# Loading the last tile of x in transfers of 5, 121 and 2 partitions instead of 5, 120 and 3

## Chip, core and metric

The kernel runs on one core of one Trainium2 chip. Five engines work side by side in a core: TensorE (PE) multiplies, VectorE (DVE), ScalarE (ACT) and GpSimd (POOL) do the elementwise work, and SyncE (SP) issues transfers. Sixteen DMA engines carry the data between the chip's main memory and the core's memory, whose 128 rows are called partitions. The metric is the device time of one execution in microseconds; the time before is the median of 3 runs.

## The reference

```python
batch, m, k, n = 16, 512, 1024, 768
x         = randn(batch, m, k)   # float32
weight    = randn(k, n)          # float32
sub_value = randn(batch, m, n)   # float32

def reference(x, weight, sub_value):
    return (np.matmul(x, weight) - sub_value).astype(np.float32)
```

With batch and m joined there are 8192 rows of x, that is 64 tiles of 128 rows. A tile of x is 128 partitions of 1024 float32, 4 KB in each partition and 512 KB in all. A tile of sub_value or of the output has 3 KB in each partition.

## The kernel before

The kernel casts each tile of x to float16 (ScalarE), transposes it (on TensorE, and for some pairs of tiles on VectorE), multiplies it by the weight (TensorE), subtracts sub_value from the product (VectorE) and stores the result. Loads and stores are listed in one order, with the kind (x, w for the weight, s for sub_value, o for the output), the first tile and the number of tiles:

```python
TRANSFERS = [
    ('x', 0, 1), ('w', 0, 1), ('x', 1, 1), ('w', 1, 1), ('x', 2, 1), ('w', 2, 1),
    # ... cut ...
    ('o', 8, 8), ('o', 16, 8), ('s', 40, 8), ('x', 48, 8), ('s', 48, 8), ('x', 56, 7), ('p', 63, 1),
    ('o', 24, 8), ('o', 32, 8), ('s', 56, 8), ('o', 40, 8), ('o', 48, 8), ('o', 56, 5),
    ('o', 61, 2), ('o', 63, 1),
]

PARTS = (120, 125), (0, 120), (125, 128)
```

All kinds but 'p' are issued by SyncE, each as one transfer over 128 partitions. Kind 'p' is tile 63 of x. GpSimd issues it, as three transfers over the ranges of partitions in PARTS, in that order, and each has a semaphore of its own:

```python
            if kind == "p":
                here, there = x_ring[:, at % NX], view(x_flat, at, 1)[:, 0]
                waits, landed["x", at] = [(counter["cast"], cast_at[at - NX]), *landed["x", at - 1]], []
                for low, high in PARTS:
                    sem = tc.alloc_semaphore(f"part{low}")
                    pool.add(lambda low=low, high=high, here=here, there=there: nc.gpsimd.dma_start(
                        out=here[low:high], in_=there[low:high], max_dma_last_dim=2048,
                    ), waits, (sem, 16))
                    landed["x", at].append((sem, 16))
                continue
```

GpSimd waits for the cast that frees the place in the ring of x tiles and for the load of x tiles 56 to 62, and then issues the three. The cast of tile 63 waits for all three semaphores:

```python
    def cast(mi):
        # ... cut ...
        waits = list(landed["x", mi])
        # ... cut: choice of the float16 buffer ...
        act.add(lambda: nc.scalar.copy(out=to, in_=x_in), waits, count("cast"))
```

The transfers that follow in SyncE's queue, the stores ('o') and the last load of sub_value ('s', 56), do not wait for tile 63. The end of the kernel is the arrival of the last store, ('o', 63, 1), at its semaphore, and of the other stores still open.

Of the kernel before, what the change touches and what calls it, by code (L numbers as in the profile page):

```python
# [35 lines left out]
    ('o', 61, 2), ('o', 63, 1),  # L36
]

PARTS = (120, 125), (0, 120), (125, 128)


class Queue:
# [65 lines left out]
def kernel(  # L108
# [134 lines left out]
    def issue():  # L243
        nonlocal known
        while todo:
# [14 lines left out]
# [5 lines that stand above are left out]
# [306 lines left out]
```

## Time and profile before

| | before |
|---|---|
| device time, median of 3 runs | 210.65 us (210.53 to 210.82) |
| span of the profiled execution | 208.6 us |
| data moved | 87.08 MB, mean 417 GB/s |
| TensorE clock granted, mean | 0.993 |
| GpSimd's three issues (line L265) | mean 668 ns each, 162.4 to 163.9 us |
| tile 63, from issue to landing | 6.8, 14.7 and 15.8 us |

The page is of one execution. It gives the busy time of each engine and, in rows of 40 digits, the busy share of each fortieth of the span (9 is 90% or more). Transfers are counted by packet, one packet being a contiguous run moved by one DMA engine; q1 is the queue of SyncE's transfers, q0 that of GpSimd's. Groups of instructions stand with their count, their mean duration and the idle time ahead of them; issues of transfers stand with the kilobytes of each and the time from issue to landing. In a row of the timeline, the first number is the start, the second the duration, both in microseconds.

### The profile page before, as it was taken

Reading aid. Unit: us, or ns where it says so; the run is one execution under the profiler, and the core shown is the slowest. Engines: PE = TensorE matmul, PEld = TensorE weight load, DVE = VectorE, ACT = ScalarE, POOL = GpSimd, SP = SyncE. Lnnn points to the kernel's source line nnn. Section 1 sums busy time; section 2 is a strip of 40 time slices with the busy share of each in tenths; the row PEclk is TensorE's granted clock in tenths of the full one; section 3 lists DMA queues with packets and bytes.
Section 4 is the critical chain, followed back from the end, with each engine's and each line's share of the span. In section 5 each row is a group of like instructions: output and inputs, shape, how many; then the busy total and the mean of one; then the engine's idle time right before and its main releaser. Section 6 shows DMA issues by size and latency. Waiting matters only on the chain.

```text
span 208.6 us, 2617 instructions
## 1 busy us (share of the span) xinstructions
PE 195.2 (94%) x1234; PEld 75.4 (36%) x700; DVE 128.1 (61%) x224; ACT 109.0 (52%) x113; POOL 3.0 (1%) x10
## 2 busy tenths in 40 slices
PE   6899699969999999999999999999999999999960
PEld 0233244324434433443443443344344344344310
DVE  2233224975993895597399389469739938942330
ACT  2655659506573761854745676183574746516300
POOL 1000000000000000000000000000000300000000
PEclk9999999999999999999999999999999999999997
DMA  6999999999999999999999999999999999999993
GB/s 204 421 428 429 437 423 431 449 435 427 424 440 446 371 443 433 444 421 411 455 440 427 415 429 448 430 452 404 424 441 428 433 432 423 443 424 433 421 418 155
DMA packets 5685, 87.08 MB, mean 417 GB/s; under 512 B 689, under 2 KB 689, under 8 KB 2097
## 3 DMA queue, kind: packets, MB, share of 16 engines
q1 hardware_dynamic: 5472, 86.51, 97.3%
q0 software_dynamic: 208, 0.52, 0.6%
q14 instruction: 4, 0.02, 0.0%
q8 instruction: 1, 0.02, 0.0%
HBM read 61.87 MB, written 25.17 MB: 417 GB/s over the span
## 4 chain that ended last, share of the span: by engine, by line
PE 75%; DMA 13%; DVE 6%; SPq 3%; issue 1%; DVEq 0%
PE po_b L200 67%; DMA so_ring<-in_sub_value_dram 13%; PE pt_b L348 8%; DVE xtp_b L381 3%; DVE so_ring L430 2%; SPq L311 2%; SPq L275 1%; SPq L566 0%; DVEq L61 0%; SPq L140 0%
## 5 line engine op out<-in xcount | busy, mean ns | idle before, releaser
L200 PE MATMUL po_b<-w_sb,xt_b 128*128 128x384 f16 x704 | 126.0, 326 | 0.9 <-DVE w_sb L278 0.8
L430 DVE TENSOR_TENSOR so_ring<-po_b,so_ring 128x768 f32<-128x768 f32 x64 | 60.7, 957 | 58.9 <-PE po_b L200 39.8
L361 ACT COPY xt_b<-pt_b 128x1024 f16<-128x1024 f16 x44 | 44.5, 1012 | 64.7 <-PE pt_b L348 63.8
L381 DVE STREAM_TRANSPOSE xtp_b<-x16p_b 32x256 f32<-32x256 f32 x144 | 62.7, 435 | 2.3
L200 PE MATMUL po_b<-w_sb,xtp_b 128*128 128x384 f16 x320 | 61.3, 326 | 1.8 <-DVE xtp_b L381 1.7
L410 PEld LDWEIGHTS <-xt_b 128*128 128x128 f16 x352 | 34.4, 98 | 58.4 <-issue 55.2
L330 ACT CAST x_b<-x_ring 128x1024 f16<-128x1024 f32 x46 | 47.2, 1048 | 5.5 <-DMA x_ring<-in_x_dram 5.5
L348 PE MATMUL pt_b<-ident,x_b 128*128 128x128 f32 x184 | 47.6, 274 | 1.9 <-ACT x_b L330 1.9
L348 PEld LDWEIGHTS pt_b<-ident,x_b 128*128 128x128 f32 x184 | 25.3, 141 | 45.0 <-issue 36.3
L330 ACT CAST x16p_b<-x_ring 128x1024 f16<-128x1024 f32 x18 | 18.8, 1046 | 14.8 <-DMA x_ring<-in_x_dram 14.8
L410 PEld LDWEIGHTS <-xtp_b 128*128 128x128 f16 x160 | 15.7, 98 | 20.3 <-issue 18.3
L278 DVE CAST w_sb<-so_ring 128x768 f16<-128x768 f32 x8 | 4.1, 557 | 12.0 <-DMA so_ring<-in_weight_dram 12.0
L200 PE MATMUL po_b<-idle_x,idle_w 128*128 128x512 f16 x26 | 7.7, 443 | 1.7 <-POOL idle_x L180 1.7
L265 POOL DMA_DIRECT2D x_ring<-in_x_dram x3 | 2.0, 668 | 136.7 <-DMA x_ring<-in_x_dram 136.7
L361 ACT COPY xtp_b<-pt_b 128x1024 f16<-128x1024 f16 x2 | 2.0, 1012 | 2.4 <-PE pt_b L348 2.4
L330 ACT ACT_TABLE_LOAD x1 | 1.3, 1283 | 0.9 <-SPq L140 0.9
L440 PEld LDWEIGHTS <-idle_w 128*128 128x128 f16 x4 | 0.4, 100 | 1.7 <-POOL idle_x L180 1.7
L189 DVE TENSOR_TENSOR ident<-along,across 32x32 f32<-32x32 f32 x4 | 0.7, 183 | 0.1
L181 DVE MEMSET ones<- 128x32 f32 x1 | 0.1, 85 | 1.0 <-SPq L140 1.0
L180 POOL MEMSET idle_x<- 128x512 f16 x1 | 0.5, 531 | 0.0
L489 POOL MEMSET mark<- 128x1 f32 x1 | 0.1, 99 | 24.0 <-ACT xtp_b L361 24.0
L512 ACT CAST stub<-ident 128x1 f16<-128x1 f32 x2 | 0.4, 194 | 0.0
(8 smaller groups left out, 1.2 us busy)
## 6 DMA issues: line engine op xcount, KB each, us to landing
so_ring<-in_sub_value_dram SPq DMA_DIRECT2D x7, 3072.0 KB, 24.2
out_dram<-so_ring SPq DMA_DIRECT2D x7, 3072.0 KB, 26.6
x_ring<-in_x_dram SPq DMA_DIRECT2D x4, 4096.0 KB, 21.6
x_ring<-in_x_dram SPq DMA_DIRECT2D x2, 2048.0 KB, 27.2
x_ring<-in_x_dram SPq DMA_DIRECT2D x1, 3584.0 KB, 21.9
so_ring<-in_weight_dram SPq DMA_DIRECT2D x4, 768.0 KB, 8.8
x_ring<-in_x_dram SPq DMA_DIRECT2D x1, 3072.0 KB, 28.3
x_ring<-in_x_dram SPq DMA_DIRECT2D x2, 1024.0 KB, 24.8
```

What stands on the lines that cost most here:

```text
L189: dve.add(lambda here=here: nc.vector.tensor_tensor(out=ident[here, here], in0=along[here], in1=across[here], op=mybir.AluOpType.is_equal, ...
L200: return nc.tensor.add_instruction(mybir.InstMatmult(name=nc.get_next_instruction_name(), engine=full.engine, ins=list(full.ins), outs=lis ...
L265: pool.add(lambda low=low, high=high, here=here, there=there: nc.gpsimd.dma_start(out=here[low:high], in_=there[low:high], max_dma_last_di ...
L275: sp.add(lambda st=st, at=at: nc.sync.dma_start(out=st, in_=w_c[at]), then=(sem, 16))
L278: lambda at=at, r=r, st=st: nc.vector.tensor_copy(out=w_sb[:, at, r], in_=st[:, r]),
L311: sp.add(lambda here=here, there=there: nc.sync.dma_start(out=here, in_=there), waits, (sem, 16))
L330: act.add(lambda: nc.scalar.copy(out=to, in_=x_in), waits, count("cast"))
L348: pe.add(lambda: nc.tensor.transpose(words, from_, ident), waits, count("turn") if last else None)
L361: act.add(lambda: nc.scalar.copy(out=to, in_=pt_b[:, b]), waits, count("evac"))
L381: dve.add(lambda: nc.vector.transpose(xt[b * Q : (b + 1) * Q, :, a * Q : (a + 1) * Q], x16[a * Q : (a + 1) * Q, :, b * Q : (b + 1) * Q],), ...
L410: pe.add(lambda weights=weights: nc.tensor.ldweights(weights, tile_position=(0, 0)), [w for w in waits if w[0] in ready])
L430: dve.add(lambda: nc.vector.tensor_tensor(out=o, in0=po[:, :, :NS], in1=o, op=mybir.AluOpType.subtract), [*landed["s", mi], (counter["mul" ...
```

## The change

The first of GpSimd's three transfers still has 5 partitions, 121 to 125 instead of 120 to 124. The second has 121, 0 to 120, instead of 120. The third has the last 2 instead of 3. The same 128 rows of 4 KB are loaded, in the same order of issue, with the same waits. The ranges determine how the rows of tile 63 are divided over the DMA engines, and that division is what the change is about.

```diff
-PARTS = (120, 125), (0, 120), (125, 128)
+PARTS = (121, 126), (0, 121), (126, 128)
```

## The prediction

> **What bounds the kernel now.** I read the page first: the share of each engine, then the row of DMA slices and the DMA queues.
>
> ```profile
> span 208.6 us, 2617 instructions
> PE 195.2 (94%) x1234; PEld 75.4 (36%) x700; DVE 128.1 (61%) x224; ACT 109.0 (52%) x113; POOL 3.0 (1%) x10
> ...
> DMA  6999999999999999999999999999999999999993
> ...
> q1 hardware_dynamic: 5472, 86.51, 97.3%
> q0 software_dynamic: 208, 0.52, 0.6%
> ```
>
> TensorE is busy for 94%, but the DMA row shows 9 in every slice except the first and the last, and SyncE's queue q1 alone fills 97.3% of 16 engines' time. GpSimd's queue q0, the one that is changed, has 208 packets and 0.6%. To see which of the two bounds holds the end, I read the timeline's last rows, then the DMA issues, and then DMA from 204 us to the end, cut into 40 slices of 0.125 us.
>
> ```profile
> 201.51 0.96 DVE L430 TENSOR_TENSOR so_ring<-po_b,so_ring 128x768 f32<-128x768 f32 x1 [1.64 <-PE po_b L200]
> ...
> out_dram<-so_ring SPq DMA_DIRECT2D x1, 384.0 KB, 4.8
> ```
>
> ```profile
> DMA  9898988882614131211111100000000000000000
> GB/s 418 344 516 344 418 369 344 344 344 98 270 74 197 49 123 74 98 74 74 74 74 49 49 0 0 0 0 0 0 0 0 0 0 0 0 0 0 0 0 0
> ```
>
> Computing ends at 201.51 + 0.96 = 202.47 us. The last store, 384 KB, lands 4.8 us after its issue, although at the 430 GB/s of the middle it is worth only 0.9 us: it stands behind stores that are still queued. In the last view all 16 engines run until about 205 us (nine slices at 8 or 9), and then fewer and fewer of them, at last one alone, until the 23rd slice, at 206.9 us. So the end is **the DMA engine with the longest backlog**. The other engines' early finish buys nothing. (The chain of waits names TensorE for 75%; it follows the last addition back and doesn't show this backlog.)
>
> The trace's packet records have start, duration and size, but no engine. I followed the 16 engines through them: on a busy engine each packet starts 3 to 4 ns before its predecessor's end. The last packets of the 16 end from 204.8 to 207.0 us: twelve by 205.8, then 206.2, 206.70, 206.76, 207.00. The lag is old: the last engine landed its share of the transfer of x tiles 40 to 47 at 114.9 us, when the middle one stood at 113.2. It isn't made up, since no engine is ever idle.
>
> Next, the part that changes: the three issues of GpSimd, DMA in the stretch from 160 to 180 us, and the cast that uses tile 63.
>
> ```profile
> x_ring<-in_x_dram POOLq DMA_DIRECT2D x1, 480.0 KB, 14.7
> x_ring<-in_x_dram POOLq DMA_DIRECT2D x1, 20.0 KB, 6.8
> x_ring<-in_x_dram POOLq DMA_DIRECT2D x1, 12.0 KB, 15.8
> ```
>
> ```profile
> DMA packets 578, 8.54 MB, mean 427 GB/s; under 512 B 124, under 2 KB 124, under 8 KB 252
> ...
> q0 software_dynamic: 208, 0.52, 6.6%
> ```
>
> ```profile
> 191.20 1.05 ACT L330 CAST x_b<-x_ring 128x1024 f16<-128x1024 f32 x1
> ```
>
> Issued from about 162 to 164 us, the three land by 179.6 us at the latest (landing of the 3-row part). The cast is at 191.2 us and has no idle time before it, so there are over 11 us of slack. The latency of the transfer doesn't matter. **What matters is which engine carries how many of its 128 rows.**
>
> **What the skill says.** The Trainium skill, "DMA: Bandwidth & Descriptors", section "Why a DMA increments its semaphore by 16 and not by 1", says that a transfer runs on k engines, the largest k up to 16 that divides the slowest dimension; for GpSimd's transfers they are k consecutive engines from a round-robin cursor. It also gives an exception: some direct copies from GpSimd take k = 16 with the partitions divided by 16 and rounded up on each engine. The section "Queues, rings and completion order" says that an engine alternates between its queues packet by packet.
>
> The trace agrees with the alternation: while q0 is active, a 24,576-byte packet of q1 and a row of q0 take turns, and the step grows from 908 to 1,063 ns. It agrees with the cursor as well. q0's 208 packets are 128 rows of 4,096 bytes, 48 of 4 bytes (3 transfers x 16 engines, the semaphore) and 32 of 8 bytes, which I call fillers. 32 = 11 + 8 + 13: one for each engine that has no row in the 5-row part, eight on the one engine without rows in the 120-row part, one for each without a row in the 3-row part. Following the packets, this one engine, X, carries one row of the 5, then eight fillers, then one row of the 3. That is a cursor: engines c to c+4, then the fifteen from c+5 on, which leaves out c+4 = X, then c+4 to c+6. So X carries 2 rows, six engines carry 9, and nine carry 8: 2 + 54 + 72 = 128. X is also a slow engine: many of its 24,576-byte packets take 945 ns where 912 is the median, so leaving it out helps.
>
> **The change part by part.** Nothing is added on any compute engine, and the bytes are the same. Only the division over engines moves. A row in the alternation costs 1,063 - 908 = 0.155 us of its engine, a filler about 914 - 908 = 0.006 us. 121 is 11 x 11, and here the skill's two rules part:
>
> - **By the divisor rule**, k = 11. Engines c+5 to c+15 carry 11 rows each, c to c+4 carry none of the 121; the cursor returns to c, and the 2-row part goes to c and c+1. Against before, the nine engines with 8 rows get +3 rows = 3 x 0.155 = +0.465 us. Engines c+5 and c+6 go from 9 to 11, +0.31 us. Engines c to c+4 carry 1 or 2 rows and end about 1 us earlier, except X, which goes from 2 rows to 1, -0.155 us.
> - The last engine before (207.00 us) has 8 rows and 2 fillers in the records, so it is one of the nine: 207.00 + 0.465 = 207.46 us. The one at 206.76 had 9 rows and can go either way; X, at 206.70, is near 206.55. So the end is +0.465 us: 210.65 + 0.465 = **211.1 us**. As the stalls that make an engine late fall differently in each run and now five engines out of 16 are relieved, +0.3 is as possible as +0.46.
>
> The 121 rows need 11 steps of 1.063 us instead of 8, 3.2 us longer: they land near 181 us instead of 177.8, still 10 us before the cast.
>
> **The rivals.**
>
> 1. *The rounded-up division.* 121 / 16 rounds up to 8 rows on each engine: 15 engines with 8, and the sixteenth, which had none, with one. If this too follows the cursor, the sixteenth is X, which then loses the row of the last part, while c+5 and c+6 get the two rows: X carries 2, six carry 9, nine carry 8, exactly as before, and the time stays at **210.65 us**. For it: 120 rows on 15 engines are what this rule gives as well (120 / 8), and the skill's exception is about direct copies, which these are. Against it: with k = 16 fixed from the lowest engine, the parts of 5 and 3 would not both meet X; the trace shows that the 120-row part moved the cursor by 15.
> 2. *X ends last.* X is slow and has stalls of its own (packets of 1,236 and 1,395 ns late in this trace), and ends only 0.3 us before the last. In runs where X is last, one row less makes the end 0.15 us earlier, until the engines with 11 rows pass it: **210.5 to 210.9 us**.
> 3. *The tile comes too late.* If 121 rows went through one engine, 121 x 1.063 = 129 us would hold up the cast: over **300 us**. Only a row count without a usable divisor would do that, and 121 has 11. I give this 1%.
>
> **Range and chances.** The divisor rule has about 65%, the rounded-up division 35%: 0.65 x 0.45 + 0.35 x 0 = +0.3 us, so 210.95 us. The range goes from 210.5 (rival 1 or 2, with runs spread as before, 210.53 to 210.82) to 211.4 (0.465 and 0.3 us of stalls on top). 2% would be 4.2 us. No part of this reaches it but rival 3, so within 2% has 0.975; slower gets 0.015 for rival 3 and what I have not seen, faster 0.01.
>
> **What the changed profile would show.** q0's packets decide between the rules. With k = 11 there are 128 rows, 48 semaphore packets and 11 + 5 x 11 + 14 = 80 fillers, **256 in all**; with rounding up, 11 + 7 + 14 = 32 fillers, **208** as before. With k = 11 the 121-row part should take some 3 us longer to land than 14.7, and the thin tail after the first engines' end should be longer by some 0.4 us, beginning earlier. Casts, additions and matmuls should keep their durations and TensorE its end near 201.5 us. The prediction is wrong if the end moves with 208 packets on q0, if the cast of tile 63 waits for its transfer, or if k = 11 shows and the time doesn't rise: then the last engine isn't one of the eleven, or isn't what sets the end.

## The result, and the profile after

| | before | after |
|---|---|---|
| device time, median | 210.64 us (210.53 to 210.82) | 211.84 us (211.60 to 212.03) |
| ratio to before | | 1.0055, 95% interval 1.0038 to 1.0073 |
| tile 63, three parts, issue to landing | 6.8, 14.7, 15.8 us | 6.6, 18.7, 19.7 us |
| last addition ends | 202.47 us | 203.62 us |

The change costs 1.2 us, by the interval 0.8 to 1.5 us. That is within 2%, but above the predicted range (210.5 to 211.4 us), with more than twice the predicted rise of 0.46 us for this division.

First the page of the kernel after: the span, the engines, the row of DMA slices and the two queues.

```profile
span 210.2 us, 2617 instructions
PE 195.8 (93%) x1234; PEld 75.5 (36%) x700; DVE 128.2 (61%) x224; ACT 108.9 (52%) x113; POOL 3.0 (1%) x10
...
DMA  6999999999999999999999999999999999999993
...
q1 hardware_dynamic: 5472, 86.51, 97.2%
q0 software_dynamic: 256, 0.53, 0.7%
```

The busy times of the engines are those of before within 0.6 us, and q1 moved the same packets. q0 has 256 packets instead of 208: 128 rows, 48 of the semaphores and 80 fillers. This is the signature that the prediction gave to the divisor rule with k = 11. The issues agree (the last two numbers of a row are the size and the median time from issue to landing):

```profile
x_ring<-in_x_dram POOLq DMA_DIRECT2D x1, 484.0 KB, 18.7
x_ring<-in_x_dram POOLq DMA_DIRECT2D x1, 20.0 KB, 6.6
x_ring<-in_x_dram POOLq DMA_DIRECT2D x1, 8.0 KB, 19.7
```

The 121 rows land 4.0 us later than the 120 rows did, where 3.2 us was predicted. No cast waits for them. The timeline has the cast of tile 63 at 192.35 us, and by then the tile has been there for some 8 us:

```profile
192.35 1.05 ACT L330 CAST x_b<-x_ring 128x1024 f16<-128x1024 f32 x1
```

Then the end, in the same view as before: DMA from 204 to 209 us in 40 slices of 0.125 us.

```profile
DMA  8885979499967979596653243110000000000000
GB/s 369 344 344 221 664 295 565 197 516 442 467 246 320 369 295 442 221 418 270 271 221 148 98 172 123 49 49 0 25 25 25 25 25 25 25 25 0 0 0 0
```

The engines stop one after the other from about 206.5 us on, and in slices 29 to 36 the rate is 25 GB/s, that of a single engine, until 208.5 us. It is the engine that ended last before, known by its lag in the packet records; I call it **L**. In these records, followed from packet to packet as in the prediction, the next-latest engines end at 207.35 us.

Where does L lose its time? The table has the time at which L finished its share of each transfer in the two profiled executions (us):

| transfer | before | after | difference |
|---|---|---|---|
| x tiles 56 to 62 | 161.85 | 162.59 | +0.74 |
| store of tiles 24 to 31 | 169.29 | 170.03 | +0.74 |
| store of tiles 32 to 39 | 177.66 | 178.70 | +1.04 |
| sub_value tiles 56 to 63 | 185.08 | 186.62 | +1.54 |
| store of tiles 40 to 47 | 192.36 | 193.89 | +1.53 |
| end | 206.99 | 208.52 | +1.53 |

The first 0.74 us is there before GpSimd issues anything (163.2 us in after), so the division of this tile can't have made it. It differs from execution to execution: the programs of nine of the experiments below are the same up to this landing but for at most one small transfer at the start, and L has it at 161.9 to 162.5 us there; before's is the earliest of all these and after's the latest. The two profiled executions also lie on opposite sides of their medians: that of after is its longest run (212.03 us, 0.19 over the median), and that of before ran 0.17 us below its median. The other 0.80 us arises while the rows of tile 63 and the load of sub_value are moved. From 185 us on, nothing is added: in every trace of this case L takes 21.9 us from its landing of this load to its end.

Within this stretch, the windows view shows where (from:to, length, then busy time of PE, PEld, DVE, ACT and POOL with counts, granted clock, DMA share, GB/s). From 168 to 175 us the rows run beside the store of tiles 32 to 39, from 176.5 to 180.5 us beside the load of sub_value tiles 56 to 63. First before, then after:

```profile
168.00:175.00 7.00, 7.00 (x49) 3.13 (x29) 3.13 (x6) 4.86 (x5) 0.00 (x0) 1.00 1.04 442
176.50:180.50 4.00, 4.00 (x28) 1.50 (x14) 3.88 (x8) 1.98 (x3) 0.00 (x0) 1.00 1.08 463
```

```profile
168.00:175.00 7.00, 7.00 (x48) 3.07 (x28) 2.92 (x6) 4.70 (x5) 0.00 (x0) 1.00 1.03 438
176.50:180.50 4.00, 4.00 (x28) 1.62 (x16) 3.88 (x9) 1.98 (x3) 0.00 (x0) 1.00 1.05 373
```

The last two numbers count. Beside the store the two kernels move data equally fast, 442 and 438 GB/s. In the next stretch the DMA engines are as busy, but move 373 instead of 463 GB/s: **each packet takes longer**. The records say which ones. Each engine has 8 packets of 24,576 bytes of the store, and 8 rows fit beside them, one by one. Of 11 rows, the last two to four run beside packets of the load on ten of the eleven engines: with the smaller parts 32 of the 128 rows, where before has 2. There most of the slowed 24,576-byte packets take 1,055 to 1,300 ns instead of 912, and not only on engines with rows: one engine whose q0 packets are all 8-byte fillers there shows 1,086, 1,300, 1,192 and 1,086 ns. A step of packet and row, 1,063 ns beside the store, takes 1,228, 1,358 and 1,252 ns here on one engine, and 1,255 ns in the mean of the 32. L itself has no row beside the load: it is the latest engine, and its eleven rows (169.9 to 178.9 us) all come before its first packet of the load. Its packets of the load are slowed all the same, as shown below. As a measure I use the **excess of the load**, the time by which its packets on an engine run over 912 ns, averaged over the 16 engines: 0.07 us before, 0.86 us after.

The load thus lands later (median of the engines 184.64 instead of 183.31 us), and the additions that need sub_value wait longer for it. Of the waits from 140 to 212 us, before and after:

```profile
DVE so_ring L430 <- DMA so_ring<-in_sub_value_dram: 2.7, 1, 2.7
```

```profile
DVE so_ring L430 <- DMA so_ring<-in_sub_value_dram: 4.1, 1, 4.1
```

The last addition ends 1.15 us later, but it doesn't set the end: after it the last store takes 5.2 us to land (4.8 before), behind the backlog.

### The profile page after: what moved, and what is told of

It is laid out like the page before. It is cut to its first block, busy times and chain, and to the rows that moved or that the text cites. A ratio compares the mean times of both kernels' runs of the same rounds, so it can differ in the third digit from the quotient of the medians.

```text
span 210.2 us, 2617 instructions
## 1 busy us (share of the span) xinstructions
PE 195.8 (93%) x1234; PEld 75.5 (36%) x700; DVE 128.2 (61%) x224; ACT 108.9 (52%) x113; POOL 3.0 (1%) x10
## 4 chain that ended last, share of the span: by engine, by line
PE 51%; DMA 35%; DVE 6%; SPq 3%; ACT 1%; issue 1%; DVEq 0%; ACTq 0%
PE po_b L200 46%; DMA so_ring<-in_sub_value_dram 21%; DMA out_dram<-so_ring 14%; PE pt_b L348 5%; DVE xtp_b L381 3%; DVE so_ring L430 3%; SPq L311 2%; SPq L275 1%; ACT xt_b L361 0%; ACT x_b L330 0%; DVEq L61 0%; SPq L566 0%; ACTq L61 0%; SPq L140 0%
## 5 line engine op out<-in xcount | busy, mean ns | idle before, releaser
L361 ACT COPY xt_b<-pt_b 128x1024 f16<-128x1024 f16 x44 | 44.5, 1012 | 66.3 <-PE pt_b L348 65.4
L361 ACT COPY xtp_b<-pt_b 128x1024 f16<-128x1024 f16 x2 | 2.0, 1012 | 2.5 <-PE pt_b L348 2.5
```

The costliest lines, as they stand in the source:

```text
L361: act.add(lambda: nc.scalar.copy(out=to, in_=pt_b[:, b]), waits, count("evac"))
```

## The experiments

Theory A: the cost comes largely from rows that run beside a load. Theory B: it comes from the division, 11 rows on L, wherever they run. Theory C, later: L stands at a known place behind the cursor, and the end moves with the rows that L gets. All ratios are to the kernel before, timed on the same chip; the chip is not the same for all experiments.

**e1: the change, issued earlier.** All rows should then run beside stores, with the same division.

```diff
-                waits, landed["x", at] = [(counter["cast"], cast_at[at - NX]), *landed["x", at - 1]], []
+                waits, landed["x", at] = [(counter["cast"], cast_at[at - NX] + 5)], []
```

> The changed kernel (parts of 5, 121 and 2), but GpSimd issues them some 7 us earlier, after the cast five tiles on, so that all 11 rows of an engine fall beside the packets of a store and none beside the load of sub_value tiles 56 to 63. Theory A (rows that spill over into the load slow that load on all 16 engines; the rest is row count): 211.1 us, that is 0.45 above before, and no 24,576-byte packets of about 1,060 to 1,200 ns between 175 and 182 us. Theory B (the division 11 x 11 itself, or its 80 fillers, costs all of it, wherever it runs): 211.8 us as the changed kernel. 256 packets on q0 in either case.

Measured: 211.88 us (211.3 to 212.4), ratio 1.0054 (1.0038 to 1.0071). The rows ran from 159.0 to 171.1 us, eight of the 128 beside the load of x tiles 56 to 62 and the others beside stores, and the excess of the load fell from 0.86 to 0.26 us, yet the time was that of after. Its load stretch:

```profile
176.50:180.50 4.00, 4.00 (x28) 1.64 (x15) 3.87 (x9) 1.98 (x3) 0.00 (x0) 1.00 0.94 406
```

406 GB/s lies between before and after. What A foresaw for the load came: none of its packets takes 1,055 to 1,300 ns (six take longer, from 181.9 us on, of which more at e6). What it foresaw for the time didn't. But the edit also moves the issue to about 155 us, into another stretch; e5 measures that by itself.

**e2: the kernel before, issued later.** The old division, with many rows beside the load.

```diff
-                waits, landed["x", at] = [(counter["cast"], cast_at[at - NX]), *landed["x", at - 1]], []
+                waits, landed["x", at] = [(counter["cast"], cast_at[at - NX] + 10)], []
```

> The kernel before (parts of 5, 120 and 3), but issued some 10 us later, so that its rows fall beside the load of sub_value tiles 56 to 63 instead of a store. Theory A: eight steps of about 0.2 us more on all engines, so 1.6 us above before, about 212.2 us, with long packets in that load. Theory B: 210.65 us, as before. The rows should still land by about 188 us, ahead of the cast at 191.

Measured: 211.57 us (211.23 to 211.99), ratio 1.0037 (1.0023 to 1.005). The rows ran from 170.4 to 182.9 us, 55 of the 128 beside the load, and the excess rose to 1.19 us. The load stretch, and the queue with its unchanged division:

```profile
176.50:180.50 4.00, 4.00 (x28) 1.50 (x14) 3.89 (x8) 1.98 (x3) 0.00 (x0) 1.00 0.94 310
```

```profile
q0 software_dynamic: 208, 0.52, 0.7%
```

With 208 packets, the old division, moving rows beside the load costs about 0.85 us (the kernel before had 210.72 us beside it) and brings the stretch down to 310 GB/s. B alone would have left the time. A's effect exists and costs time, though less than expected. L pays for rows that are not its own: one of its eight runs beside the load, yet its load packets run over by 0.82 us, where before has 0.15.

**e3: one transfer of 128 partitions.** Eight rows on each engine, X among them, no fillers.

```diff
-PARTS = (120, 125), (0, 120), (125, 128)
+PARTS = ((0, 128),)
```

> One transfer of 128 partitions instead of three, at the time of before. Both theories expect 16 engines with 8 rows each, 144 packets on q0 without fillers, and no spill. The slow engine X gets 8 rows instead of 2, so it ends 6 x 0.155 = 0.9 us later less some 0.2 us of fillers saved, near 207.4 us in the span of before: about 211.1 us. If the imbalance of rows costs nothing, 210.65 us.

Measured: 210.89 us (210.41 to 211.56), ratio 1.0008 (1.0001 to 1.0015). q0 has 144 packets, 128 + 16, and 512 KB landed in 13.8 us:

```profile
q0 software_dynamic: 144, 0.52, 0.6%
```

```profile
x_ring<-in_x_dram POOLq DMA_DIRECT2D x1, 512.0 KB, 13.8
```

In the trace L ends last, with 8 rows. X, which now has 8 too and is known by its packets of some 940 ns, ends at 206.0 us; it was expected near 207.4. So sparing X, as the kernel before does, is worth 0.2 us, by the interval 0.0 to 0.3 us.

**e4: the change, with rows 20 KB apart in main memory.** A variant of A: in after, the rows of tile 63 lie 32 KB apart in main memory, and at that pitch they might collide with each other or with the load's addresses. This kernel reads 128 other rows of x into tile 63, so it doesn't compute the last tile of the reference; sizes, division and order are unchanged.

```diff
-                here, there = x_ring[:, at % NX], view(x_flat, at, 1)[:, 0]
+                here, there = x_ring[:, at % NX], x_flat[56 * P : 61 * P].rearrange("(p j) c -> p j c", j=5)[:, 0]
```

(with PARTS as changed)

> The changed kernel at its own time, but GpSimd's rows are read 20 KB apart instead of 32 KB (they are other rows of x than tile 63's, so the output of that tile is not the reference's). If the spilled rows slow the load because rows 32 KB apart meet in main memory (theory A1), the long packets go and the time is about 211.1 us. If the cause is in the engines or on the side of the core's memory (theory A2), or is theory B, it stays at 211.8 us.

Measured: 211.96 us (211.48 to 212.04), ratio 1.0053 (1.004 to 1.0065), excess 0.95 us, 365 GB/s in the load stretch (373 after). So this pitch of the rows isn't the cause. From its landing of the store of tiles 24 to 31 to that of the load, L takes 0.82 us longer than in before, so this part of the loss recurs.

**e5: the kernel before, issued early as in e1.** The control for e1.

```diff
-                waits, landed["x", at] = [(counter["cast"], cast_at[at - NX]), *landed["x", at - 1]], []
+                waits, landed["x", at] = [(counter["cast"], cast_at[at - NX] + 5)], []
```

> The kernel before (5, 120 and 3), issued as early as the early run of the changed kernel. If row count on the engine that ends last (theory C: one engine, L, is the last in every trace, and three rows more on it are three rows more on the end) and rows beside loads are all there is, the time is 210.7 us, as before, since L has 8 rows here. If issuing early costs by itself, 211.3 us or more, and the early run of the changed kernel says nothing against theory A.

Measured: 211.12 us (210.77 to 211.54), ratio 1.0018 (1.001 to 1.0027).

```profile
176.50:180.50 4.00, 4.00 (x28) 1.64 (x15) 3.87 (x9) 1.98 (x3) 0.00 (x0) 1.00 1.08 467
```

The load runs at full rate (467 GB/s, excess 0.14 us), and still the time is about 0.4 us up. Issuing early has a cost of its own, which spoils e1 as a test of A by its time alone. Between the kernels of e1 and e5 only the division differs: 0.0036 in ratio, about 0.76 us, with an uncertainty of about 0.39 us (they ran on two chips, each against before).

**e6: the change, issued one cast later than e1.** To repeat the comparison with e5 at nearly the same place.

```diff
-                waits, landed["x", at] = [(counter["cast"], cast_at[at - NX]), *landed["x", at - 1]], []
+                waits, landed["x", at] = [(counter["cast"], cast_at[at - NX] + 6)], []
```

(with PARTS as changed)

> The changed kernel (5, 121 and 2) issued one cast later than in the early run (some 3 us), so that the rows begin after the load of x tiles 56 to 62 and end before that of sub_value: beside stores alone. Theories A and C: 211.15 us (row count only, 0.465 us over before). If the division itself or its fillers cost the rest, 211.8 us.

Measured: 211.91 us (211.63 to 212.2), ratio 1.0065 (1.0051 to 1.0078). Rows from 159.8 to 171.9 us, seven beside the load of x tiles 56 to 62 and the others beside stores, excess 0.31 us.

```profile
176.50:180.50 4.00, 4.00 (x27) 1.59 (x15) 3.89 (x8) 1.98 (x3) 0.00 (x0) 1.00 0.98 418
```

Against e5 it is +0.79 us by the medians (by the ratios 0.99, with an uncertainty of 0.34 us); three rows by the prediction's 0.155 us give 0.47. So eleven rows on L cost time even where no row runs beside the load of sub_value. The two traces show only the three rows: from its landing of x tiles 56 to 62 to its end L takes 45.57 us in e5 and 45.99 in e6, 0.42 us more. What fills the rest isn't shown. L also stalls in this load, at 182 to 184 us, and this varies from trace to trace: single packets run over by 1.05 us in e1, 0.71 in e6, 0.75 in e5, 0.62 in e3, 0.42 in e9, 0.15 in before and nothing in e8. In after, e2 and e4, where the load was slow on all engines, there is no such stall. What triggers it isn't shown.

**e7: small parts that show the cursor.** Six rows, five times two, then 112 rows, which fall beside the load.

```diff
-PARTS = (120, 125), (0, 120), (125, 128)
+PARTS = (0, 6), (6, 8), (8, 10), (10, 12), (12, 14), (14, 16), (16, 128)
```

> Tile 63 in parts of 6, five times 2, and 112 partitions, at the time of before. By the divisor rule with a cursor the first six transfers use engines c to c+5, c+6 and c+7, and so on up to c+14 and c+15, and the 112 rows all sixteen, 7 each. So the part in which L has a row instead of a filler tells which pair of engines L belongs to; X must have its row in the first part. Each engine has 8 rows. Time near 211 us, as with one transfer of 128 partitions.

Measured in one execution: 212.56 us (before there: 210.66). The load stretch, and the queue with 128 rows, 7 x 16 semaphore packets and 80 fillers:

```profile
176.50:180.50 4.00, 4.00 (x28) 1.50 (x14) 3.88 (x8) 1.98 (x3) 0.00 (x0) 1.00 1.01 361
```

```profile
q0 software_dynamic: 320, 0.53, 0.8%
```

Each engine got one row of the first six parts: 6 + 5 x 2 = 16 consecutive engines, so the cursor carries on from part to part. X is in the first part, as it should be. L stands at c+10 or c+11; the records, which have no engine number, don't decide. With 108 of the 128 rows beside the load, the excess is 1.28 us, the highest of all kernels, and 16 x (24,576 + 4,096) bytes take a step of about 1.30 us, 353 GB/s. For the pure load it is 16 x 24,576 bytes in 0.912 us, 431 GB/s, and for the store with rows 16 x (24,576 + 4,096) in 1.063 us, 431 GB/s as well.

**e8 and e9: the kernel before, after a small transfer that should move the cursor.** Eight bytes to 6 or 7 partitions at the start, so that the 120 rows leave out another engine than X. GpSimd also waits for this transfer before it issues the three parts.

```diff
+    spare = sbuf("spare", [P, 2], F32)
+    turned = tc.alloc_semaphore("turned")
+    pool.add(lambda: nc.gpsimd.dma_start(out=spare[:6], in_=x_flat[:6, :2]), then=(turned, 16))
```

(e9 with 7 in place of 6)

> The kernel before (5, 120 and 3), but GpSimd first loads 8 bytes into each of 6 partitions at the kernel's start. That moves the cursor by 6, so the 120-row part leaves out engine c+10 instead of X. From the parts run, L is c+10 or c+11. Theory C (the engine L sets the end): if L is c+10, it has 2 rows instead of 8, ends 0.9 us earlier, and the next engines (X with 8 rows, about 206.9 us) set the end: 210.0 to 210.5 us, below before. If L is c+11, it keeps 8 or 9 rows and X has more: 210.9 to 211.1 us. If L is not what sets the end, both shifts give the same.

> The same with 7 partitions, so that engine c+11 is left out. Theory C: 210.0 to 210.5 us if L is c+11, 210.9 to 211.1 us if L is c+10. One of the two shifts should be faster than the other by 0.5 us or more, and in its trace L should carry 2 rows.

Measured: 210.75 us, ratio 1.0 (0.999 to 1.0011), and 210.76 us, ratio 1.0001 (0.9991 to 1.001). Neither tests C: in both traces the engine left out is still X, recognised by fillers 938 to 952 ns apart. The small transfer did not move the cursor. Why, is open; it may be that it was divided by the second rule of the prediction, over all 16 engines, which these runs don't tell apart. In e8's trace L, with its 8 rows, is not the last: it ends at 207.05 us, and the engine that was second in before ends at 207.21.

**e10: a first large part of 117 rows.** k = 13 with 9 rows, a division between 8 and 11.

```diff
-PARTS = (120, 125), (0, 120), (125, 128)
+PARTS = (117, 122), (0, 117), (122, 128)
```

> Parts of 5, 117 and 6 at the time of before. 117 = 13 x 9, so by the divisor rule 13 engines carry 9 rows (L among them), q0 has 128 + 48 + 48 = 224 packets, and one row of each, plus the 6-row part, falls beside the load. Theories A and C: L is 0.155 us later by its ninth row and about 0.16 us by the part beside the load, so 210.9 to 211.1 us, between before and the changed kernel. If the division 11 x 11 is special, 210.65 us.

Measured: 210.89 us (210.38 to 211.5), ratio 1.0005 (0.9994 to 1.0015). q0 has the packets of k = 13, 128 + 48 + 48:

```profile
q0 software_dynamic: 224, 0.52, 0.6%
```

```profile
176.50:180.50 4.00, 4.00 (x28) 1.56 (x15) 3.89 (x8) 1.98 (x3) 0.00 (x0) 1.00 1.00 395
```

One row more than the store has packets already shows in the load (eight rows beside it, excess 0.46 us, 395 GB/s), but no more than 0.3 us of time. L has no row there, and its load packets run over by 0.12 us only.

**e11 and e12: leave out L.** First parts of 11 or 12 rows turn the cursor by 11 or 12, so that the 15 engines of the 105 rows leave out c+10 or c+11.

```diff
-PARTS = (120, 125), (0, 120), (125, 128)
+PARTS = (105, 116), (0, 105), (116, 128)
```

(e12: (105, 117), (0, 105), (117, 128))

> Parts of 11, 105 and 12 at the time of before. 105 = 15 x 7, and the 11 rows ahead of it move the cursor to c+11, so the 105 leave out engine c+10, which has 2 rows in all; X (c+4) has 9, the others 8 or 9; q0 has 192 packets. Nothing but a last row each falls beside the load. Theory C (L ends last and its rows count): if L is c+10, it ends 0.9 us earlier, the time is 210.1 to 210.6 us, and the engine left out in the trace is not X but L. If L is c+11, it is 210.9 to 211.1 us, a little above the single transfer of 128.

> Parts of 12, 105 and 11: the same, with engine c+11 left out. Theory C: 210.1 to 210.6 us if L is c+11, 210.9 to 211.1 us if L is c+10. If both are alike, the end is not set by L's rows, or L is neither.

Measured: 210.92 us (210.56 to 211.29), ratio 1.0006 (0.9999 to 1.0012), and 210.81 us (210.28 to 210.95), ratio 0.9998 (0.9989 to 1.0006). In e11's trace it is the late engine that carries two rows, so L is c+10. It still ends last, at 207.14 us: six rows fewer save it 0.93 us, but its last packet of the store of tiles 32 to 39 (1,196 ns) and two of the load (1,444 and 1,040 ns) run over 912 by 0.94 us in all, where before has 0.15. Behind it are the engine that ended at 206.76 us before (206.94) and X (206.59), each with 9 rows. In e12 L has 8 rows again and ends last, at 207.14 us. So L's place is found, but the end did not follow its rows as C has it. Even without the stalls little was to be gained: L leads by 0.24 us only in before, and the 128 rows must go somewhere. No division tried beats before.

Over all traces, the excess of the load goes with the number of rows beside it. With up to 4 of the 128 rows there it is 0.07 to 0.31 us, nearly all of it single stalls; with 7 rows (e11) 0.29, 8 (e10) 0.46, 32 (after) 0.86, 34 (e4) 0.95, 55 (e2) 1.19 and 108 (e7) 1.28.

## Why the prediction was wrong, step by step

- **The end is the engine with the longest backlog:** right. The last engine of after is L, alone for a microsecond; the later last addition (+1.15 us) is hidden behind the backlog. The lag is old, too: the two landings that the prediction gives for it, 114.9 and 113.2 us, are 114.6 and 112.9 in the records, 1.7 us apart as well.
- **The division:** right. 256 packets are the divisor rule; the rounding of rival 1 is refuted. The Trainium skill, "DMA: Bandwidth & Descriptors", section "Why a DMA increments its semaphore by 16 and not by 1", has both rules; here 120, 121, 117 and 105 rows went by the divisor (15, 11, 13, 15 engines), of which 121 and 117 tell the rules apart.
- **Three rows more on L, +0.465 us:** this part is in the trace. L is one of the eleven, its eleven rows come before its packets of the load, and each costs it the predicted 0.155 us. The sum failed because it ended there. The failing step is "A row in the alternation costs 1,063 - 908 = 0.155 us of its engine": the price had been read beside a store, and a row was to cost its own engine alone. Of the 128 rows, 32 run beside the load, with steps of 1,255 ns in the mean, and the load's packets slow on all engines. L's three load packets that were slowed by the rows of others took 1,094 + 1,012 + 1,095 = 3,201 ns, where 3 x 912 = 2,736: another 0.465 us. With 0.15 us of a stall that before had in this load and after did not, the sum is 0.465 + 0.465 - 0.15 = 0.78 us, against 0.80 us between the landings of L. That stall is a matter of the execution: in e8 and e9, with the parts and the time of before, L's packets of this load run over by 0 and 0.42 us, and in e4, the repetition of after, by 0.50. So the slow load adds to L something between 0.05 and 0.5 us, net of such stalls.
- **What stays open:** 1.2 us minus 0.8 us. The 0.74 us ahead of the rows in after's profile doesn't fill this gap, since it arises before GpSimd issues: in after's trace eight packets of the load of x tiles 56 to 62 stall by 160 to 360 ns at 157.8 to 160.3 us, against at most one in any other. Nor is it shown that the slow load and the 1.2 us are one and the same thing: each alone costs time (e2: about +0.85 us for the place; e6 against e5: +0.79 us for the division), but taking the slow load away by an earlier issue (e1, e6) doesn't bring the time back. Part of that is the cost of issuing early (e5, +0.4 us), itself unexplained.
- **Rival 2, X ends last, one row less helps:** didn't happen. L was last, and X's lead was of no use. **Rival 3, the tile comes too late:** excluded, 8 us of slack remain.
- **The range:** three runs of before spread by 0.3 us, and I took this for the spread of the kernel. Over all its runs on record it is 210.17 to 211.33 us. And 0.3 us was allowed for everything that the sum lacked, while one neglected interaction alone was 0.465 us in the trace.

## What to carry to other kernels

When transfers are nearly always queued, count rows per DMA engine and not bytes: of the row counts tried here, 121 put 11 rows on eleven engines, 120 eight on fifteen, and the last engine's lag was never made up. Then count what these rows run beside. A row of a second stream cost its engine 0.155 us beside a store, and 0.35 us (after) to 0.44 us (e2) in the mean beside a load, where other engines paid too, L with no row of its own there. So the duration of a step must come from the stretch in which it will run, and the sum must include the engines that get no row. That the rows are best no more than the packets of a neighbour that takes them well (eight here) fits these runs, but 117 rows, nine on an engine, cost too little to prove it. And one trace of each kernel is not enough for tenths of a microsecond: L's stalls in one load range from 0 to 1.05 us.

## What was not expected of the hardware

- Rows from GpSimd beside a store cost only their bytes (431 GB/s with and without them); beside a load the sum falls to about 353 GB/s, and engines without rows slow as well. Whether main memory, the core's memory or something between them is the cause wasn't tried; a pitch of 20 KB instead of 32 changed nothing (e4). The Trainium skill's section "Queues, rings and completion order" has the alternation of queues that these steps show, with no price for it.
- The fillers are real packets: one engine without rows gets as many 8-byte packets as the others get rows. They cost little (6 ns a step), but they make the division readable: 208, 224, 256 and 144 packets.
- Single packets stall by 140 to 1,255 ns around a change between store and load. In the traces with hardly a row beside the load, the long packets of the store of tiles 32 to 39 (at 173.7 to 176.1 us, X's 1,236 ns in before is one of them) are all the last of their engine's eight, and those of the load from 181 us on are among the last three. Some come when all 16 engines are still in the same transfer, so it is not only that others have moved on. This is an association in the traces; it was not tested by an experiment.
- A GpSimd transfer of 48 or 56 bytes at the start left the cursor where it was (e8, e9).
